# A hybrid attention block: the compressed branch's steps at other slots, and the stream's pieces run in pairs

## The chip, the core and the metric

The kernel runs on one core of one Trainium2 chip. The metric is the device time of one execution in microseconds, as the median of several; a profile of one more execution shows what each engine did. The engines are named as the profile names them: PE (TensorE's matmuls), PEld (its weight loads), DVE (VectorE), ACT (ScalarE), POOL (GpSimd), SP (SyncE, which only issues transfers here).

## The reference, cut to what matters

One layer of a decoder trunk on 512 tokens of width 2048, in float32. A normalised `h` goes through one wide input projection; its columns feed a sparse attention (mixer A) and a gated MLP (mixer B); both are merged, projected and added back. What the change touches is in mixer A, for 16 heads in 4 groups with head size 64:

```
kc, vc = compress(k_c), compress(v_c)            # 31 compressed keys and values per group
sc  = q . kc * scale - slope * distance          # compressed scores, masked
p_c = softmax(sc) ;  o_c = p_c . vc
o_s = softmax(q . k_s ...) . v_s                 # selected blocks: all 8 of them at this length
o_w = softmax(q . k_w ...) . v_w                 # window of 512: all causal keys
o   = gate0 * o_c + gate1 * o_s + gate2 * o_w
```

At 512 tokens the top-16 selection takes all 8 blocks, so the selected and the window branch are both plain causal attention, over different keys and values.

## The kernel before, in words

**Matmuls in three parts.** Each float32 operand is split into a high and a low part (`high` at L158 on ACT, `low` at L164 on DVE), and a product is three matmuls: high by high, low by high, high by low. The large projections are jobs of one generator, `gemm`. One step of it, called a unit or piece of the stream here, is such a triple of 128x512 matmuls (L425 to L427 for the jobs that run during the attention: the query and gate projections `q2` to `q7` and `za0` to `za7`). `fill(n)` runs the next n units.

**The attention** runs over 48 slots: 8 tiles `ft` of two heads each, and in each tile six slots j = 0 to 5, for the query blocks i = 3, 3, 2, 2, 1, 0. Slots 0 to 3 take one branch each, slots 4 and 5 both branches at once. What happens to a slot is spread over four slots: `scores` (L1262, L1263: two pairs of matmuls into two PSUM banks `ps_s`, then on DVE the bias and row maximum at L1266, which empties the bank), `exponentials` on ACT in the same slot (L1275), `weigh` on DVE one slot later (L1286, L1291), `transpose_probs` on PE two slots later (L1316 into `ps_t`, emptied by a cast to `pth` on ACT and a subtraction to `ptl` on DVE), `values` three slots later (L1335, L1336 into `ps_o`).

**The compressed branch** works on a group of four heads, that is on a pair of tiles, one pair ahead. Its steps are events in between: `cmp_keys` (POOL), `cmp_scores` (L1371: two halves of two matmuls, each half in a bank `ps_c`, emptied by a copy on ACT at L1372 and an addition on DVE at L483), `cmp_softmax` (transposes L1383, copy L1386, then DVE and ACT), `cmp_weigh`, `cmp_transpose` (transposes L1413 into `ps_c`, copy `pc` L1415 on ACT, two casts, two subtractions on DVE), and `cmp_values` once per tile (L1425 into `ps_c`, copy `oc` L1427).

**Banks.** PSUM has eight banks here, two for each of four tags. `ps_s` and `ps_c` share the two banks with tag "s"; `ps_t` has the two of "t", `ps_o` those of "o", the stream's jobs those of "g" in this stage. A new tile of a tag takes the bank of the last but one, and its first matmul waits until that one has been emptied.

**The order** is written out by hand. For each slot the main loop (`for s in range(n + 3)`) makes a list of events. PE's events are each preceded by `flush()`, which issues what was deferred (the `low` parts, the additions), and followed by `fill` with a number of units. A running credit sets that number: the units of the attention, 224 less 19, are spread evenly over the events on PE. Each engine runs its own instructions in the order in which they were issued.

## Time and profile before

| | |
|---|---|
| median of 3 runs | 1517.71 us (1517.4 to 1518.03) |
| the profiled execution | 1518.42 us, of it 1516.7 us span |
| granted TensorE clock | 0.999 |
| PE busy | 1504.3 us, 99% of the span |
| DVE, ACT, POOL busy | 1217.1, 853.9, 375.0 us |
| DMA | 340.5 MB, mean 225 GB/s |
| the attention's slots | about 215 to 476 us of the span |

The span is the time from the first to the last instruction; the profiled execution's own time has 1.7 us around it. In a row of the profile's timeline stand the start, the duration and the engine of an instruction, its line and the tiles that it writes and reads, and in brackets how long the engine was idle before it and who ended that. Matmuls overlap: the time that one costs is the distance from its start to the next one's, 0.23 us for 512 columns, not the duration that is printed, 0.39.

### The profile page before, as it was taken

To read this page: it belongs to the slowest core of one execution; us is meant where nothing else is said; L and a number is where in the kernel's file an instruction comes from. 1 tells how busy PE (TensorE), PEld (TensorE's weight loads), DVE (VectorE), ACT (ScalarE), POOL (GpSimd) and SP (SyncE) were. 2 spreads that over 40 slices of the span, in tenths; PEclk is the share of its full clock that TensorE was granted. 3 is DMA by queue.
4 is the path that set the end of the run, shared out by engine and by line. 5 is a ranking of instruction groups with operands and counts; after the bars stand their busy time and mean duration, and the time that the engine had idled before them with its cause. 6 is when DMAs were issued, how large, how long until landed. Compare 5 with 4: busy or idle time off the path is not lost.

```text
span 1516.7 us, 20626 instructions
## 1 busy us (share of the span) xinstructions
PE 1504.3 (99%) x7269; PEld 1262.3 (83%) x7269; DVE 1217.1 (80%) x1871; ACT 853.9 (56%) x1488; POOL 375.0 (25%) x595
## 2 busy tenths in 40 slices
PE   9999999999999999999999999999999999999997
PEld 8889988888888888888888888888888888888886
DVE  7557768899997888978887878797877985677877
ACT  6544456767675555555655555555556565444556
POOL 1311223323432233333333333421110002100000
PEclk9999999999999999999999999999999999999999
DMA  8686879778875895968686968896797879955555
GB/s 314 202 167 198 235 158 217 176 159 224 180 189 194 271 288 139 301 154 282 145 265 177 267 176 263 231 317 250 265 323 245 248 187 330 314 169 182 182 209 191
DMA packets 187351, 340.54 MB, mean 225 GB/s; under 512 B 12520, under 2 KB 84848, under 8 KB 184048
## 3 DMA queue, kind: packets, MB, share of 16 engines
q0 software_dynamic: 67216, 168.42, 41.1%
q1 hardware_dynamic: 119888, 170.55, 35.5%
q8 instruction: 57, 0.93, 0.3%
q14 instruction: 46, 0.38, 0.1%
q10 hardware_dynamic: 144, 0.26, 0.0%
HBM read 278.88 MB, written 109.58 MB: 256 GB/s over the span
## 4 chain that ended last, share of the span: by engine, by line
PE 95%; ACT 2%; DVE 2%; DMA 1%; issue 0%; POOL 0%; DVEq 0%; SPq 0%; ACTq 0%; POOLq 0%
PE ps_m L399 7%; PE ps_m L400 7%; PE ps_m L401 7%; PE ps_wo L400 3%; PE ps_wo L401 3%; PE ps_wo L399 3%; PE ps_t L1316 2%; PE ps_za L427 2%; PE ps_za L425 2%; PE ps_za L426 2%; PE ps_q L425 2%; PE ps_q L427 2%; PE ps_q L426 2%; PE ps_u L399 2%; PE ps_u L401 2%; PE ps_ub L401 2%
## 5 line engine op out<-in xcount | busy, mean ns | idle before, releaser
L164 DVE TENSOR_TENSOR ls<-b,hs 128x1024 fp32r<-128x1024 f32 x218 | 266.5, 1223 | 107.5 <-ACT hs L158 106.4
L158 ACT CAST hs<-b 128x1024 fp32r<-128x1024 f32 x218 | 229.2, 1053 | 195.0 <-PE ps_m L401 43.1
L158 ACT CAST hs<-raw 128x1024 fp32r<-128x1024 f32 x114 | 120.0, 1055 | 116.9 <-issue 34.1
L164 DVE TENSOR_TENSOR ls<-raw,hs 128x1024 fp32r<-128x1024 f32 x114 | 139.3, 1222 | 38.7 <-ACT hs L158 38.5
L164 DVE TENSOR_TENSOR lo<-raw,hi 128x512 fp32r<-128x512 f32 (+1 forms) x152 | 100.8, 669 | 36.9 <-issue 9.9
L158 ACT CAST hi<-raw 128x512 fp32r<-128x512 f32 (+1 forms) x152 | 89.8, 601 | 56.8 <-PE ps_pg L440 10.6
L399 PE MATMUL ps_m<-hs,act_h 128*128 128x512 f32 x256 | 100.2, 391 | 0.0
L400 PE MATMUL ps_m<-ls,act_h 128*128 128x512 f32 x256 | 99.7, 389 | 0.0
L401 PE MATMUL ps_m<-hs,act_l 128*128 128x512 f32 x256 | 99.7, 389 | 0.0
L282 DVE TENSOR_TENSOR b<-raw,b 128x1024 f32<-128x1024 f32 x72 | 87.8, 1219 | 3.0 <-DMA raw<-in_w_in_dram 2.9
L282 DVE TENSOR_TENSOR b<-b,b 128x1024 f32<-128x1024 f32 x72 | 87.7, 1219 | 0.0
L158 ACT CAST pth<-ps_t 128x512 fp32r<-128x512 f32 (+1 forms) x88 | 47.8, 544 | 58.7 <-PE ps_t L1316 58.2
L1275 ACT ACTIVATE prob<-prob,st 128x512 f32<-128x512 f32 (+3 forms) x128 | 70.7, 555 | 2.6 <-DVE st L1266 2.4
L164 DVE TENSOR_TENSOR ptl<-ps_t,pth 128x512 fp32r<-128x512 f32 (+1 forms) x88 | 56.1, 637 | 14.5 <-ACT pth L158 13.8
L358 POOL COPY pad_r<-pad_r 128x1 f32<-128x1 f32 x42 | 31.0, 737 | 136.1 <-ACT pad_r L357 136.1
L1266 DVE CUSTOM_DVE_ANT_0 prob<-ps_s,b 128x512 f32<-128x512 f32 (+3 forms) x128 | 56.2, 485 | 1.9 <-PE ps_s L1263 1.5
L401 PEld LDWEIGHTS ps_m<-hs,act_l 128*128 128x128 f32 x256 | 48.1, 188 | 10.0
L400 PEld LDWEIGHTS ps_m<-ls,act_h 128*128 128x128 f32 x256 | 48.1, 188 | 9.8
L399 PEld LDWEIGHTS ps_m<-hs,act_h 128*128 128x128 f32 x256 | 48.1, 188 | 9.9
L425 PE MATMUL ps_za<-act_h,hi 128*128 128x512 f32 x128 | 53.7, 420 | 0.0
L1291 DVE TENSOR_SCALAR prob<-prob,st,gates 128x512 f32<-128x512 f32 (+3 forms) x128 | 51.5, 455 | 1.8
L425 PE MATMUL ps_q<-act_h,hi 128*128 128x512 f32 x128 | 52.2, 408 | 0.0
(704 smaller groups left out, 4556.4 us busy)
## 6 DMA issues: line engine op xcount, KB each, us to landing
raw<-in_w_in_dram SPq DMA_DIRECT2D x112, 512.0 KB, 5.6
b<-in_w_in_dram SPq DMA_DIRECT2D x56, 512.0 KB, 7.2
o<-in_w_out_dram POOLq DMA_DIRECT2D x48, 512.0 KB, 8.0
t<-in_w_up_b_dram POOLq DMA_DIRECT2D x24, 512.0 KB, 8.1
raw<-in_w_ple_gate_dram SPq DMA_DIRECT2D x24, 512.0 KB, 3.8
b<-o SPq DMA_DIRECT2D x18, 512.0 KB, 6.5
o<-o POOLq DMA_DIRECT2D x16, 512.0 KB, 4.9
act_l<-gate POOLq DMA_DIRECT2D x8, 1024.0 KB, 12.8
```

The costliest lines, as they stand in the source:

```text
L158: nc.scalar.copy(hi, src)
L164: nc.vector.tensor_tensor(out=lo, in0=src, in1=hi.bitcast(F32), op=ALU.subtract)
L282: nc.vector.tensor_tensor(out=b[o], in0=b[x], in1=b[y], op=ALU.subtract)
L399: nc.tensor.matmul(o, ah, wh, start=st, stop=False, skip_group_check=go)
L400: nc.tensor.matmul(o, ah, wl, start=False, stop=False, skip_group_check=go)
L401: nc.tensor.matmul(o, al, wh, start=False, stop=sp, skip_group_check=go)
L425: nc.tensor.matmul(ps, hi[:, j], ah, start=st, stop=False)
L426: nc.tensor.matmul(ps, hi[:, j], al, start=False, stop=False)
L427: nc.tensor.matmul(ps, lo[:, j], ah, start=False, stop=sp)
L1266: nc.vector.tensor_tensor_reduce(out=pt[:, j * n:j * n + n], in0=o[:, j], in1=b0[:, 512 - n:], scale=-SLOPE[h], scalar=3.0e38, op0=ALU.add ...
L1275: nc.scalar.activation(sl, sl, AF.Exp, bias=st[:, 0, j, hh:hh + 1], scale=-1.0, accum_out=st[:, 1, j, hh:hh + 1])
L1291: nc.vector.tensor_scalar(out=sl, in0=sl, scalar1=st[:, 1, j, hh:hh + 1], scalar2=gates[:, i, gate:gate + 1], op0=ALU.mult, op1=ALU.mult)
```

## The change

- `cmp_scores` does one half now (`a` = 0 or 1) and is an event twice: in slot 4 and in slot 5 of an odd tile, where both halves were one event of slot 5. Its work on POOL (`vcb`) goes with the second half.
- `cmp_values` of an even tile is the last event of slot 5, behind the second transposes and values. In odd tiles it stays in slot 3.
- The number of units after an event is no longer the whole part of the credit: below two (and with no `cmp_transpose` next), it is two after the scores if the credit is positive, and none after another event.

```
-    def cmp_scores(g):
-        for ft in (2 * g, 2 * g + 1):
-            finish(f"q{ft}")
-        t = pct_t["s"] = ring(1, F32)[:, 0]
-        halves = slice(0, 64), slice(64, 128)
-        for a in range(2):
-            b = bank("s", "ps_c")
-            for r in range(2):
-                nc.tensor.matmul(b, kcp[:, 32 - 32 * r:160 - 32 * r], qs[4 * g + 2 * a + r], start=r == 0, stop=r == 1)
-            nc.scalar.copy(t[halves[a]], b[halves[1 - a]])
-            deferred.append(partial(add, t[halves[a]], t[halves[a]], b[halves[a]]))
+    def cmp_scores(g, a):
+        finish(f"q{2 * g + a}")
+        if not a:
+            pct_t["s"] = ring(1, F32)[:, 0]
+        t, b, halves = pct_t["s"], bank("s", "ps_c"), (slice(0, 64), slice(64, 128))
+        for r in range(2):
+            nc.tensor.matmul(b, kcp[:, 32 - 32 * r:160 - 32 * r], qs[4 * g + 2 * a + r], start=r == 0, stop=r == 1)
+        nc.scalar.copy(t[halves[a]], b[halves[1 - a]])
+        deferred.append(partial(add, t[halves[a]], t[halves[a]], b[halves[a]]))
+        if a:
+            cmp_parts(g)
+
+    def cmp_parts(g):
         for r in range(4):
...
     cmp_keys(0)
-    for f, u in zip((cmp_scores, cmp_softmax, cmp_weigh, cmp_transpose), (4, 3, 4, 7)):
+    fill(4)
+    flush()
+    cmp_scores(0, 0)
+    for f, u in zip((partial(cmp_scores, a=1), cmp_softmax, cmp_weigh, cmp_transpose), (0, 3, 4, 7)):
...
-            if ft % 2 == 1 and ft < 7 and j == 5:
-                events.append((cmp_scores, (ft + 1) // 2))
+            if ft % 2 == 1 and ft < 7 and j >= 4:
+                events.append((cmp_scores, (ft + 1) // 2, j - 4))
...
-            if j == (3 if ft % 2 else 5):
+            if ft % 2 and j == 3:
                 events.append((cmp_values, ft))
...
         events += tq[1:] + vq[1:]
+        if s < n and ft % 2 == 0 and j == 5:
+            events.append((cmp_values, ft))
...
-                units = max(int(credit) + ahead, e[0] is scores)
+                units = int(credit) + ahead
+                if units < 2 and not ahead:
+                    units = 2 if e[0] is scores and credit > 0 else 0
                 fill(units)
                 credit -= units
```

What this does to the order is seen at three places. In the rows, `x4` counts equal instructions that follow each other; L1369 of the changed kernel is L1371 of the one before, L1370 is L1372, L1415 is L1413, L1417 is L1415 and L1427 is L1425.

**The compressed scores.** PE in slot 5 of tile 1, before, from the first transposes to the second:

```order
L1316 MATMUL ps_t<-ident,prob 128x128 x4
L1335 MATMUL ps_o<-pth,vt 128x256
L1336 MATMUL ps_o<-ptl,vt 128x256
L1335 MATMUL ps_o<-pth,vt 128x256
L1336 MATMUL ps_o<-ptl,vt 128x256
L425 MATMUL ps_q_2913<-act_h_88,hi 128x512
L426 MATMUL ps_q_2913<-act_l_89,hi 128x512
L427 MATMUL ps_q_2913<-act_h_88,lo 128x512
L1371 MATMUL ps_c<-b_2371,kcp 128x512 x2
L1371 MATMUL ps_c<-b_2634,kcp 128x512 x2
L1316 MATMUL ps_t<-ident,prob 128x128 x2
```

PE in slot 4 of tile 1, now, from the unit before the first transposes to the second:

```order
L425 MATMUL ps_za_2637<-act_h_94,hi 128x512
L426 MATMUL ps_za_2637<-act_l_95,hi 128x512
L427 MATMUL ps_za_2637<-act_h_94,lo 128x512
L1316 MATMUL ps_t<-ident,prob 128x128 x4
L1335 MATMUL ps_o<-pth,vt 128x256
L1336 MATMUL ps_o<-ptl,vt 128x256
L1335 MATMUL ps_o<-pth,vt 128x256
L1336 MATMUL ps_o<-ptl,vt 128x256
L1369 MATMUL ps_c<-b_2371,kcp 128x512 x2
L1316 MATMUL ps_t<-ident,prob 128x128 x2
```

The first half has moved from slot 5 to slot 4, and the second half stands the same way in slot 5. The unit between the values and the compressed scores is gone; two units stand between the scores and the first transposes (the second of them is shown), and two behind the second values. ACT at the same place, before (slot 5) and now (slots 4 and 5):

```order
L158 CAST pth<-ps_t 128x512
L1275 ACTIVATE prob,st<-prob,st 128x128 x4
L158 CAST hi<-raw 128x512
L1372 COPY b_2922<-ps_c 64x512 x2
L158 CAST pth<-ps_t 128x256
```

```order
L158 CAST pth<-ps_t 128x512
L1275 ACTIVATE prob,st<-prob,st 128x256 x4
L1370 COPY b_2856<-ps_c 64x512
L158 CAST pth<-ps_t 128x256
L611 ACTIVATE o_580<-ps_za_2637 128x512
L158 CAST hi<-raw 128x512
L158 CAST pth<-ps_t 128x512
L1275 ACTIVATE prob,st<-prob,st 128x128 x4
L1370 COPY b_2856<-ps_c 64x512
L158 CAST pth<-ps_t 128x256
```

The copies stand alone now, each directly behind the slot's four exponentials; the cast of weights (`hi<-raw`) that stood between is elsewhere in the slot.

**The compressed probabilities' transposes.** PE in slot 4 of tile 4, from these transposes on, before and now:

```order
L1413 MATMUL ps_c<-ident,b_3737 128x128 x4
L1316 MATMUL ps_t<-ident,prob 128x128 x2
L1335 MATMUL ps_o<-pth,vt 128x256
L1336 MATMUL ps_o<-ptl,vt 128x256
L1335 MATMUL ps_o<-pth,vt 128x256
L1336 MATMUL ps_o<-ptl,vt 128x256
L425 MATMUL ps_q_3999<-act_h_90,hi 128x512
L426 MATMUL ps_q_3999<-act_l_91,hi 128x512
L427 MATMUL ps_q_3999<-act_h_90,lo 128x512
L1262 MATMUL ps_s<-ob_h,b_3174 128x256
```

```order
L1415 MATMUL ps_c<-ident,b_3656 128x128 x4
L1316 MATMUL ps_t<-ident,prob 128x128 x2
L1335 MATMUL ps_o<-pth,vt 128x256
L1336 MATMUL ps_o<-ptl,vt 128x256
L1335 MATMUL ps_o<-pth,vt 128x256
L1336 MATMUL ps_o<-ptl,vt 128x256
L1262 MATMUL ps_s<-ob_h,b_3174 128x256
```

The unit behind the last values is gone; it stands ahead of the slot's first transposes now.

**The compressed values of an even tile.** PE in slot 5 of tile 4, before, from the compressed values to the next slot's scores, and now, from the same values on:

```order
L1425 MATMUL ps_c<-b_4091,vcb 128x512 x2
L425 MATMUL ps_q_3999<-act_h_92,hi 128x512
L426 MATMUL ps_q_3999<-act_l_93,hi 128x512
L427 MATMUL ps_q_3999<-act_h_92,lo 128x512
L1316 MATMUL ps_t<-ident,prob 128x128 x2
L1335 MATMUL ps_o<-pth,vt 128x256
L1336 MATMUL ps_o<-ptl,vt 128x256
L425 MATMUL ps_q_3999<-act_h_92,hi 128x512
L426 MATMUL ps_q_3999<-act_l_93,hi 128x512
L427 MATMUL ps_q_3999<-act_h_92,lo 128x512
L1262 MATMUL ps_s<-ob_h,b_3448 128x512
```

```order
L1335 MATMUL ps_o<-pth,vt 128x256
L1336 MATMUL ps_o<-ptl,vt 128x256
L1427 MATMUL ps_c<-b_4091,vcb 128x512 x2
L1262 MATMUL ps_s<-ob_h,b_3448 128x512
L1263 MATMUL ps_s<-ob_l,b_3448 128x512
L1262 MATMUL ps_s<-ob_h,b_3448 128x512
```

Two units, the second transposes and the values now stand ahead of the compressed values, and the next slot's scores directly behind them.

## The prediction

> **What bounds the kernel now.** I read the page first, then the stretch of the attention, then its waits, then the order of events at the places that the waits name.
>
> ```profile
> span 1516.7 us, 20626 instructions
> PE 1504.3 (99%) x7269; PEld 1262.3 (83%) x7269; DVE 1217.1 (80%) x1871; ACT 853.9 (56%) x1488; POOL 375.0 (25%) x595
> ```
>
> TensorE sets the end: it has work in 99% of the span, and the change neither adds nor removes one of its instructions. It moves instructions only inside the attention, which is this stretch:
>
> ```profile
> 215.00:476.00 261.00, 259.37 (x1476) 220.99 (x1476) 234.50 (x650) 180.98 (x482) 90.27 (x129) 1.00 0.81 187
> ```
>
> The columns are the stretch, its length, and the busy time of PE, PEld, DVE, ACT and POOL. PE is full, VectorE has 234.5 of 261 us, ScalarE 181. So the change can win only what PE loses here by waiting, and it can lose by making PE wait more. Where PE loses time, and what ScalarE waits for:
>
> ```profile
> ACT pth L158 <- PE ps_t L1316: 58.2, 31, 2.8
> PEld ps_s L1262 <- DVE b L483: 3.0, 6, 0.6
> PE ps_c L1425 <- DVE st L1266: 0.9, 3, 0.3
> ```
>
> The second and third row are the places: six waits of the scores (L1262) for the additions that empty the compressed scores' bank (L483), and three of the compressed values (L1425) for a bank that the scores before them still hold. All are waits for one of the two banks with tag "s". The first row matters most for the change: ScalarE's cast of transposed probabilities is first in its queue in a slot, and it waits for PE's transposes.
>
> One of the three places of the first kind, in order of time. "Zero" below is always the start of the first stream unit after a slot's scores.
>
> ```profile
> 268.52 0.27 PE L1262 MATMUL ps_s<-ob_h,b 128*128 128x256 f32 x1
> ...
> 268.98 0.40 PE L425 MATMUL ps_za<-act_h,hi 128*128 128x512 f32 x1
> 269.69 0.60 PE L1316 MATMUL ps_t<-ident,prob 128*128 128x128 f32 x4
> 270.38 0.59 ACT L158 CAST pth<-ps_t 128x512 fp32r<-128x512 f32 x1
> 270.60 0.39 PE L425 MATMUL ps_q<-act_h,hi 128*128 128x512 f32 x1
> 270.86 0.41 ACT L1275 ACTIVATE prob<-prob,st 128x128 f32<-128x128 f32 x1
> 271.29 1.09 PE L1371 MATMUL ps_c<-b,kcp 128*128 128x512 f32 x4
> 272.22 0.38 PE L1316 MATMUL ps_t<-ident,prob 128*128 128x128 f32 x2
> 272.41 0.60 ACT L158 CAST hi<-raw 128x512 fp32r<-128x512 f32 x1
> 273.04 1.19 ACT L1372 COPY b<-ps_c 64x512 f32<-64x512 f32 x2
> 273.66 1.40 DVE L483 TENSOR_TENSOR b<-b,ps_c 64x512 f32<-64x512 f32 x2 [0.22 <-ACT b L1372]
> 273.83 0.39 PE L427 MATMUL ps_q<-act_h,lo 128*128 128x512 f32 x1
> 274.40 0.50 PE L1262 MATMUL ps_s<-ob_h,b 128*128 128x512 f32 x1 [0.18 <-DVE b L483]
> 275.12 0.50 PE L1262 MATMUL ps_s<-ob_h,b 128*128 128x512 f32 x1
> 275.69 0.40 PE L425 MATMUL ps_q<-act_h,hi 128*128 128x512 f32 x1
> ```
>
> The reader sees a chain on ScalarE that hangs on PE's transposes: zero 268.98, transposes +0.71, cast +1.40, first exponential +1.88, the four of 128 columns over at +3.43 (0.39 each), a cast of weights, the copies at +4.06, the first addition at +4.68. The scores start 0.74 us after an addition has started (273.66 to 274.40; they were due 0.34 earlier, since 273.83 + 0.23 = 274.06). From 273.83 to 275.69 PE takes 1.86 us for one matmul and four of 0.23, that is 1.15: 0.71 us lost.
>
> **What the change moves, and what each piece costs.** Steps on PE between zero and later events are read off these rows: one stream unit 0.69 (three matmuls of 0.23), the first transposes and the values after them 0.91 (269.69 to 270.60; 0.35 + 0.09 is the transposes' part), a half of the compressed scores 0.46 (271.29 to 272.22 for two), two transposes 0.22, the short values 0.23, the long ones 0.47, a pair of scores 0.46 at 128 columns (268.52 to 268.98), 0.92 at 512. From transposes to cast 0.69, from cast to exponentials 0.48.
>
> *Pairing of the units.* The bare gain of fewer changes between kinds of matmul is nothing to count: a unit's last matmul takes the same 0.23 whether values, scores or another unit follow. What does change: after the scores now two units run before the transposes, not one. PE's slot is not longer for it, but the cast starts at 1.38 + 0.69 = +2.07 instead of about +1.40, and everything behind it in ScalarE's queue is 0.69 later, while the next slot's scores are due when they were. In a plain slot this is covered: the scores' two banks are emptied by VectorE a slot ahead, and the transposes' banks come round a slot later. Where ScalarE empties an "s" bank, nothing covers it. These places follow.
>
> *Compressed scores, now half in slot 4, half in slot 5 (three times).* Slot 4: cast +2.07, exponentials +2.55, four of 256 columns in 1.99 (next fence, 363.68 to 365.67), so the copy goes at +4.54, now directly behind them; addition 0.62 later, +5.16; bank free for the scores 0.74 later, +5.90. The scores that need it are the second of slot 5: 0.91 + 0.46 + 0.22 + 0.47 + four units 2.76 + 0.23 = +5.05. Wait 0.85, and 0.1 for starting again (274.40 + 0.23 against the 0.33 that it took): 0.95. Slot 5: exponentials end at 2.55 + 1.55 = +4.10, addition +4.72, free +5.46; due 0.91 + 0.46 + 0.22 + 0.23 + 2.76 + 0.46 = +5.04: 0.42 + 0.1 = 0.52. Together 1.47 where 0.71 was lost; three times, **+2.3 us**. Each wait is for one copy and one addition now, not two, but there are two of them. PE runs in order, so the rest of the slot stands behind each, and ScalarE and VectorE wait for it in turn. Behind the first addition on VectorE stand the low parts of the second transposes and the next slot's maxima; the maxima start with the late scores anyway, so that is covered by the same wait.
>
> *The compressed probabilities' transposes (L1413), not moved by name, but moved by the pairing (three times).* They take an "s" bank that ScalarE copies out:
>
> ```profile
> 361.82 0.40 PE L425 MATMUL ps_q<-act_h,hi 128*128 128x512 f32 x1
> 362.51 0.60 PE L1316 MATMUL ps_t<-ident,prob 128*128 128x128 f32 x4
> 363.20 0.59 ACT L158 CAST pth<-ps_t 128x512 fp32r<-128x512 f32 x1 [2.09 <-PE ps_t L1316]
> 363.68 0.51 ACT L1275 ACTIVATE prob<-prob,st 128x256 f32<-128x256 f32 x1
> 364.79 0.60 PE L1413 MATMUL ps_c<-ident,b 128*128 128x128 f32 x4
> 365.67 0.60 ACT L158 CAST hi<-raw 128x512 fp32r<-128x512 f32 x1
> 366.18 0.58 ACT L1415 COPY pc<-ps_c 128x512 f32<-128x512 f32 x1
> 366.73 0.28 PE L1263 MATMUL ps_s<-ob_l,b 128*128 128x256 f32 x1
> 366.85 0.34 PE L1262 MATMUL ps_s<-ob_h,b 128*128 128x256 f32 x1
> ```
>
> Here the chain ends in a dead heat: the copy starts at +4.36 and the second scores start 0.67 later, at +5.03, as soon as PE gets to them. Moving the cast from +1.38 to +2.07 makes that a wait of 0.66 to 0.69, with the restart 0.75, at the two later places (same units, same weights' cast in the queue). At the first place (tile 2) that cast is out of the way (0.51 less), but the unit that stood behind the transposes is gone as well: free at 2.55 + 1.99 + 0.67 = +5.21, due 1.38 + 0.91 + 0.69 + 0.44 + 0.22 + 0.47 + 0.23 = +4.34, 0.87 and 0.1. Together 2.5 against 0.1 to 0.2 now: **+2.3 us**.
>
> *The compressed values of even tiles, now last in slot 5 (three times).* Before:
>
> ```profile
> 369.21 0.39 PE L427 MATMUL ps_q<-act_h,lo 128*128 128x512 f32 x1
> 369.27 0.28 DVE L1266 CUSTOM_DVE_ANT_0 prob<-ps_s,b 128x128 f32<-128x128 f32 x1
> 369.92 0.71 PE L1425 MATMUL ps_c<-b,vcb 128*128 128x512 f32 x2 [0.31 <-DVE st L1266]
> 370.46 0.40 PE L425 MATMUL ps_q<-act_h,hi 128*128 128x512 f32 x1
> ...
> 306.72 0.57 ACT L1427 COPY oc<-ps_c 128x512 f32<-128x512 f32 x1
> ...
> 283.55 0.71 ACT L1275 ACTIVATE prob<-prob,st 128x512 f32<-128x512 f32 x1
> ```
>
> 369.21 to 370.46 is 1.25 us for 0.69 of work: 0.56 lost, because VectorE is late with the maxima. At the slot's end that wait is gone (three times 0.56, -1.7). But now the next scores come directly behind, and the second of them needs the same bank that the values have just filled. ScalarE's queue: exponentials end +4.10, cast of the second transposes 0.36, cast of weights 0.51, copy 0.57 and the 0.08 to the release: +5.62. Due 1.38 + 0.91 + 0.22 + 1.38 + 0.23 + 0.46 + 0.46 = +5.04. Wait 0.58, with the restart 0.68; three times +2.0. Net **+0.3 us**.
>
> *The rest.* The starting steps ahead of the slots keep PE's order. In odd tiles the compressed values stand as far from zero as they did (two units, transposes, values). POOL's and SP's queues keep what they issue. The softmax transposes of the third tile pair come later in their slot: 2.55 + 1.42 for two exponentials of 512 columns (0.71 in the last row) + 0.51 + 0.65 against a due time of +4.93, about 0.2.
>
> **Sum**: +2.3 + 2.3 + 0.3 + 0.2 = +5.1 us on the profiled execution's 1518.4 us (its span is 1516.7), so 1523.5. That execution lies 0.7 above the median of 1517.7, so I forecast **1522.8 us**.
>
> Bounds: the gain cannot exceed what PE loses at the places, 3 x 0.71 + 3 x 0.56 and the small ones of about 0.5, so 4.3 us. Each of the new waits is the difference of two times of about 5 us, at twelve places; 0.1 us off in ScalarE's chain is 1.2 us in the sum. I take 0.25 as the error of a chain put together from parts (the cast of weights counts 0.51 and may stand on either side): 3 us either way.
>
> A rule that speaks for the pairing: the Trainium skill, Perfetto Trace Analysis, section Matmul Optimizations, says that the array's power follows its use, so matmuls ought to run back to back in batches. The trace leaves it nothing to win: the granted clock of the stretch is 1.00 above, with the singles. By the rule the sum would stay as it is, since what it asks for is granted already.
>
> **The rivals.**
>
> *The waits vanish (faster).* Half the compressed scores per slot, and values that no longer meet late maxima: if every release came before its due time, PE would gain up to 4.3 us, about 1513.7. For it: the values' wait does go, and the copy loses the second copy ahead of it. Against it: it needs ScalarE's chain to start at +1.40 as before, and the first fence of waits shows the chain's head waiting for the transposes 31 times. It decides at a chain 0.7 us shorter than in my sum. 8%.
>
> *A draw.* The chain runs 0.4 us shorter than I put it, say because the casts of weights fall into the wait for the transposes everywhere. Then the scores' waits come to 0.55 and 0.12, the transposes' to 0.57 and twice 0.35, the values' to 0.28: 2.0 + 1.3 + 0.8 = 4.1 against 4.0 now, about 1518. For it: these casts move between slots in the changed order. Against it: I have put each one where the order has it. 24%.
>
> *VectorE becomes the bound (slower still).* It is 90% busy here, and with the second cast later it idles ahead of the low parts and catches up in the next slot. Around the softmax of even tiles it has the reductions on top; if its lateness then reaches the transposes' banks, by up to the 0.69 us that the chain is later, in one or two slots of each of three tile pairs, another 2 to 4 us come on top: 1526. For it: 26.5 us of slack over 48 slots is 0.55 each, less than 0.69. Against it: the banks come round a slot later. 10%.
>
> **How the numbers follow.** The likeliest, 58%, has its own range 1519.8 to 1525.8. A change of 0.2% is 3.0 us, about what a measurement of this kernel tells from none. One tenth of the likeliest case falls inside that; of the draw, one tenth lies beyond it on either side; of the first rival an eighth stays inside. Slower: 0.52 + 0.02 + 0.10 = 0.64; within: 0.06 + 0.19 + 0.01 = 0.26; faster: 0.07 + 0.03 = 0.10. The range from 1516.3 to 1526.5 takes in the draw, the bounds and half of the third rival.
>
> **What would show it.** In the changed profile's waits: the scores (L1262) wait for the compressed scores' addition six times, in slots 5 and 0, about 0.85 and 0.4 each; they wait for ScalarE's copies pc and oc, which they do nowhere now; the compressed values no longer wait for the maxima. In order of time the first cast of a slot starts 2.07 us after zero. If the pc and oc copies release nobody, the chain on ScalarE is not what binds, and the first rival holds. If the transposes wait for the low parts in many slots, the third does. If PE's loss in the stretch stays near 4 us, it is the draw.

## The result, and the profile after

| | before | after |
|---|---|---|
| median | 1517.63 us (6 runs, 1517.4 to 1518.03) | 1528.77 us (6 runs, 1528.22 to 1529.39) |
| ratio | | 1.0074, 95% interval 1.0063 to 1.0084 |
| the profiled execution, its span | 1518.42, 1516.7 us | 1528.22, 1526.4 us |
| granted clock | 0.999 | 0.998 |
| PE's loss in the attention (215 to 487 us) | 4.35 us | 16.29 us |

The change costs 11.1 us; I had forecast 5.1 and a range that ends at 1526.5. "Loss" here and below is worked out from PE's rows as in the prediction: the distance from the start of a matmul to the start of the next, less the time that its columns take (0.23 us for 512), added up where it is above 0.035. By places:

| PE waits at | before | my sum | after |
|---|---|---|---|
| the scores behind the compressed scores (add) | 2.3 | 4.4 | 5.1 |
| the scores behind the compressed probabilities' transposes (`pc`) | 0.1 | 2.5 | 2.9 |
| the scores behind the even tiles' compressed values (`oc`) | 0 | 2.0 | 1.9 |
| the even tiles' compressed values (maxima) | 1.7 | 0 | 0 |
| the softmax transposes of the third pair | 0 | 0.2 | 0.3 |
| the transposes, for a low part (`ptl`) | 0.2 | 0.2 | 4.3 |
| the odd tiles' compressed values (maxima) | 0 | 0 | 1.8 |
| small ones | 0.1 | 0.1 | 0.1 |

By the pages of the two profiles PE is busy for 1505.2 us (1504.3 before), so the work is the same; the 9.7 us of span are waiting, and the chain of work that sets the end runs over ScalarE and VectorE for 4% of the span each where it was 2% each (PE 89% for 95%). PE's loss grew by 11.9 us, the attention from its first scores to its last values by 11.0 (262.4 to 273.4 us); in these two executions the stretch ahead of it was 1.0 us shorter after the change, the stretch behind it 0.3. The waits of PE in the attention of the changed kernel:

```profile
PE ps_s L1262 <- DVE b L483: 3.5, 6, 0.8
PE ps_t L1316 <- DVE ptl L164: 3.1, 4, 1.0
PE ps_s L1262 <- ACT pc L1417: 2.0, 3, 0.9
PE ps_s L1262 <- ACT oc L1429: 1.0, 3, 0.4
PE ps_c L1427 <- DVE st L1266: 0.9, 3, 0.5
```

The first, third and fourth row are the waits of my sum, six, three and three as said. The second and the last are not in it. The fences below show rows picked from a view, in order of time; the rows between them are left out. A place of the first kind, the changed kernel in slot 4 of tile 3:

```profile
331.79 0.39 PE L425 MATMUL ps_za<-act_h,hi 128*128 128x512 f32 x1
333.85 0.59 ACT L158 CAST pth<-ps_t 128x512 fp32r<-128x512 f32 x1 [2.60 <-PE ps_t L1316]
334.33 0.51 ACT L1275 ACTIVATE prob<-prob,st 128x256 f32<-128x256 f32 x1
336.43 0.58 ACT L1370 COPY b<-ps_c 64x512 f32<-64x512 f32 x1
337.05 0.68 DVE L483 TENSOR_TENSOR b<-b,ps_c 64x512 f32<-64x512 f32 x1 [1.89 <-ACT b L1370]
337.79 0.39 PE L1262 MATMUL ps_s<-ob_h,b 128*128 128x256 f32 x1 [0.79 <-DVE b L483]
```

Zero is 331.79, the cast starts at +2.06 (forecast +2.07), the copy at +4.64 (forecast +4.54), the addition at +5.26 (+5.16). VectorE stands idle for 1.89 us ahead of the addition: it is not VectorE that is late there, but what it is given.

The wait that I had put at nothing, the compressed values of an odd tile (slot 3 of tile 3). Before:

```profile
321.43 0.60 PE L1316 MATMUL ps_t<-ident,prob 128*128 128x128 f32 x4
322.57 0.34 PE L1262 MATMUL ps_s<-ob_h,b 128*128 128x384 f32 x1
322.68 0.68 DVE L164 TENSOR_TENSOR lo<-raw,hi 128x512 fp32r<-128x512 f32 x1
322.91 0.59 ACT L158 CAST pth<-ps_t 128x512 fp32r<-128x512 f32 x1
323.28 0.41 DVE L1351 TENSOR_TENSOR o<-o,ps_o 64x256 f32<-64x256 f32 x1
324.16 0.69 DVE L164 TENSOR_TENSOR ptl<-ps_t,pth 128x512 fp32r<-128x512 f32 x1
324.76 0.55 DVE L1266 CUSTOM_DVE_ANT_0 prob<-ps_s,b 128x384 f32<-128x384 f32 x1
325.56 0.63 PE L1425 MATMUL ps_c<-b,vcb 128*128 128x512 f32 x2
```

and after:

```profile
324.24 0.60 PE L1316 MATMUL ps_t<-ident,prob 128*128 128x128 f32 x4
324.59 0.42 PE L1262 MATMUL ps_s<-ob_h,b 128*128 128x384 f32 x1
325.22 0.41 DVE L1351 TENSOR_TENSOR o<-o,ps_o 64x256 f32<-64x256 f32 x1 [0.18 <-ACT o L1348]
325.74 0.58 ACT L158 CAST pth<-ps_t 128x512 fp32r<-128x512 f32 x1
326.10 0.69 DVE L164 TENSOR_TENSOR lo<-raw,hi 128x512 fp32r<-128x512 f32 x1
326.82 0.69 DVE L164 TENSOR_TENSOR ptl<-ps_t,pth 128x512 fp32r<-128x512 f32 x1
327.43 0.55 DVE L1266 CUSTOM_DVE_ANT_0 prob<-ps_s,b 128x384 f32<-128x384 f32 x1
328.04 0.72 PE L1427 MATMUL ps_c<-b,vcb 128*128 128x512 f32 x2 [0.20 <-DVE st L1266]
```

The first row of each is the *second* transposes of the slot before. They stood 1.14 us ahead of the next scores, with a unit in between; now they stand 0.35 ahead. Their cast starts 0.34 us after the scores' start before, 1.15 after. But their low part (`ptl`) does not follow the cast directly: in both kernels VectorE first makes two additions on `o` (L1351, L1352), for which ScalarE copies `o`. These start 0.71 us after the scores' start before and 0.63 now, so they are not late. What is new ahead of `ptl` is the low part of weights (`lo<-raw,hi`, 0.7 us): it stood ahead of the additions, at +0.11, and now stands behind them, at +1.51. So `ptl` starts at +2.23 for +1.59, and the maxima, which stand behind it in VectorE's queue, at +2.84 for +2.19. The compressed values are due at about the same distance as before (2.99, now 3.1), but the bank comes free later: 0.46 us lost.

### The profile page after: what moved, and what is told of

Read it like the earlier page. It is cut to its first block, busy times and chain, and to the rows that moved or that the text cites. A ratio compares the mean times of both kernels' runs of the same rounds, so it can differ in the third digit from the quotient of the medians.

```text
span 1526.4 us, 20639 instructions
## 1 busy us (share of the span) xinstructions
PE 1505.2 (99%) x7269; PEld 1262.3 (83%) x7269; DVE 1220.2 (80%) x1871; ACT 856.1 (56%) x1488; POOL 379.4 (25%) x595
## 4 chain that ended last, share of the span: by engine, by line
PE 89%; ACT 4%; DVE 4%; DMA 1%; issue 1%; POOL 0%; DVEq 0%; ACTq 0%; POOLq 0%
PE ps_m L400 7%; PE ps_m L399 7%; PE ps_m L401 7%; PE ps_wo L400 3%; PE ps_wo L401 3%; PE ps_wo L399 3%; ACT prob L1275 2%; PE ps_u L401 2%; PE ps_ub L399 2%; PE ps_u L400 2%; PE ps_pg L401 2%; PE ps_pg L399 2%; PE ps_ua L400 2%; PE ps_zb L400 2%; PE ps_zb L399 2%; PE ps_vn L400 2%
## 5 line engine op out<-in xcount | busy, mean ns | idle before, releaser
L164 DVE TENSOR_TENSOR ls<-b,hs 128x1024 fp32r<-128x1024 f32 x218 | 266.6, 1224 | 107.8 <-ACT hs L158 106.8
L164 DVE TENSOR_TENSOR ls<-raw,hs 128x1024 fp32r<-128x1024 f32 x114 | 139.4, 1223 | 39.2 <-ACT hs L158 38.9
L164 DVE TENSOR_TENSOR lo<-raw,hi 128x512 fp32r<-128x512 f32 (+1 forms) x152 | 101.1, 670 | 37.4 <-issue 8.7
L358 POOL COPY pad_r<-pad_r 128x1 f32<-128x1 f32 x42 | 34.4, 820 | 132.3 <-ACT pad_r L357 132.3
L164 DVE TENSOR_TENSOR ptl<-ps_t,pth 128x512 fp32r<-128x512 f32 (+1 forms) x88 | 55.5, 637 | 13.4 <-ACT pth L158 12.2
L1316 PE MATMUL ps_t<-ident,prob 128*128 128x128 f32 x320 | 49.5, 274 | 3.1 <-DVE ptl L164 3.1
```

Source lines behind the costliest of these rows:

```text
L164: nc.vector.tensor_tensor(out=lo, in0=src, in1=hi.bitcast(F32), op=ALU.subtract)
L358: nc.gpsimd.tensor_copy(steps[:, 16 + i:17 + i], steps[:, i:i + 1])
L1316: nc.tensor.transpose(b[:, (2 * e + hh) * P:(2 * e + hh + 1) * P], pts[hh][:, c:c + P], ident)
```

## The experiments

All ratios stand against the kernel before as measured beside each run (1517.6 to 1517.9 us). "Tile pair" is two tiles, 12 slots.

| run | what differs | median us | PE's loss us |
|---|---|---|---|
| before | | 1517.63 | 4.35 |
| after | | 1528.77 | 16.29 |
| e1 | pairs alone | 1526.09 | 13.85 |
| e2 | moved steps alone | 1519.57 | 5.97 |
| e3 | after, exponentials ahead of the first transposes | 1526.07 | 13.21 |
| e4 | before, the same | 1522.28 | 8.87 |
| e5 | before, one unit first, the rest in pairs | 1522.08 | 8.93 |
| e6 | before, two units first, the rest single | 1523.67 | 10.89 |
| e7 | before, even tiles' values last | 1517.39 | 4.05 |
| e8 | moved steps, compressed scores in "t" banks | 1519.14 | 5.73 |
| e9 | after, copies ahead of the exponentials | 1527.90 | 15.42 |
| e10 | moved steps, copies ahead of the exponentials | 1518.73 | 5.28 |
| e11 | before, copies ahead of the exponentials | 1517.47 | 3.94 |
| e12 | after, less VectorE work at the softmax | 1525.98 | 13.00 |
| e13 | after, less VectorE work in each slot | 1525.71 | 13.30 |
| e14 | before, the same | 1517.38 | 3.92 |
| e15 | after, as e9 and e13 together | 1522.64 | 10.39 |
| e16 | before, more ScalarE work in each slot | 1521.95 | 8.48 |
| e17 | after, weight casts on GpSimd | 1525.14 | 13.01 |
| e18 | before, weight casts on GpSimd | 1514.79 | 1.30 |

### Which part of the change costs

**e1, the pairs alone**

```
-                units = max(int(credit) + ahead, e[0] is scores)
+                units = int(credit) + ahead
+                if units < 2 and not ahead:
+                    units = 2 if e[0] is scores and credit > 0 else 0
```

> The kernel before, with the new rule for the stream's pieces alone (two at a time, none in between); the compressed steps stay where they were. Theory A (the pairing makes the first transposes of a slot about 0.69 us later, and with them ScalarE's cast, exponentials and copies and VectorE's second low part): the waits at the compressed scores and at the compressed probabilities' transposes are there, and the transposes wait for the low parts; PE loses 12 to 16 us in the attention where it lost 4.35, so about 1525 to 1529 us. Theory B (the other places of the compressed steps are what costs): PE loses 4 to 6 us, 1517 to 1520 us. Theory C (the two costs need each other): in between, 1520 to 1524 us.

Measured: 1526.09 us, ratio 1.0055 (1.0042 to 1.0067).

**e2, the moved steps alone** (the change with these lines taken back)

> The changed kernel with the old rule for the pieces (one behind the scores, the rest one at a time); the compressed scores stay spread over two slots and the even tiles' compressed values stay last in theirs. Theory A: the first cast of a slot starts about 1.4 us after the slot's first scores, each half of the compressed scores waits 0.3 us at most, the even tiles' values wait no more for the maxima; PE loses 1 to 4 us, so 1514.5 to 1517.5 us. Theory B: the places cost by themselves, PE loses 10 us or more, 1523 to 1528 us. Theory C: 1518 to 1522 us.

Measured: 1519.57 us, ratio 1.0011 (1.0002 to 1.0020). **e7**, of the moves only the even tiles' values:

```
-            if j == (3 if ft % 2 else 5):
+            if ft % 2 and j == 3:
                 events.append((cmp_values, ft))
...
         events += tq[1:] + vq[1:]
+        if s < n and ft % 2 == 0 and j == 5:
+            events.append((cmp_values, ft))
```

> The kernel before with one part of the change alone: the even tiles' compressed values last in their slot. From the run with all the moves (PE loses 5.97, of it 1.23 at the copies behind these values and 3.96 at the spread scores): the three waits for the maxima (1.65 with their small ends) go, three waits for the copy of about 0.45 come, PE loses 3.9 to 4.2, 1517 to 1518.2 us. Then the spread of the compressed scores alone is worth +1.5 to +2 us. If the two moves need each other's lateness, this one comes out below 1516.5 or above 1518.5.

Measured: 1517.39 us, ratio 0.9996 (0.9987 to 1.0005).

The pairs cost 8.2 us, the moves 1.7, together 9.9 of the 11.1. Of the moves the values' place is worth nothing that can be measured (three waits of 0.55 for three of 0.43 to 0.49), so the spread of the compressed scores is what costs, about 2. My expectation for e2 (0.3 us a half) was wrong: in slot 4 the halves still wait 0.84 to 1.15 us, because in front of the copy stand the cast, four exponentials of 256 columns (2.0 us, 1.55 in slot 5) and a cast of weights; two halves wait where both halves together waited once.

### What about the pairs

**e5, one unit behind the scores, the rest in pairs**, and **e6, two behind the scores, the rest single** (both with the compressed steps where they were):

```
+                units = int(credit) + ahead
+                if e[0] is scores:
+                    units = 1
+                elif units < 2 and not ahead:
+                    units = 0
```

```
-                units = max(int(credit) + ahead, e[0] is scores)
+                units = max(int(credit) + ahead, 2 * (e[0] is scores))
```

> The kernel before, compressed steps where they were, with one piece behind the scores as before and all other pieces in pairs or threes. It tells apart whether pairs as such cost, or the second piece between the scores and the first transposes. Theory A (the second piece ahead of the first transposes): the first cast of a slot starts 1.4 us after the slot's first scores, as before; PE loses 3.5 to 5.5 us in the attention (4.35 before, 13.85 with all pieces in pairs), 1517 to 1519 us. Theory D (pieces in pairs are what costs, wherever they stand): PE loses 9 to 14 us, 1522 to 1526 us.

> The other half: the kernel before with two pieces behind the scores and the rest one at a time. Theory A: first cast at 2.07 us, the waits at the compressed probabilities' transposes (about 0.8 to 1.2 each) and the transposes' waits for the low parts (about 1.2 in tiles 2 and 4) are there; PE loses 11 to 15 us, 1524 to 1527 us. Theory D: one pair a slot of two, so a half of the loss at most: 7 to 9 us, 1520 to 1522 us.

Measured: 1522.08 (1.0027, 1.0016 to 1.0038) and 1523.67 (1.0035, 1.0022 to 1.0049). Neither theory is right alone. PE's waits in e5 and in e6:

```profile
PE ps_t L1316 <- DVE ptl L164: 2.1, 3, 0.7
PE ps_s L1262 <- DVE st L1266: 1.2, 1, 1.2
```

```profile
PE ps_t L1316 <- DVE ptl L164: 2.4, 2, 1.4
PE ps_s L1262 <- DVE b L483: 2.4, 3, 1.0
PE ps_c L1425 <- DVE st L1266: 2.0, 4, 1.1
```

In e6 the first cast is late, and the compressed scores lose 0.9 to 1.6 us each. But the odd tiles' compressed values lose 0.05 at most, where e1 and the changed kernel lose 0.46 to 0.75 in three tiles: with single units there is still a unit behind the second transposes at a slot's end. (The last row is the even tiles' values, 0.54 to 0.56 each as before, and 1.3 in tile 0.) In e5 the first cast is on time and these values lose 0.1 at most, but the second transposes of three slots lose 0.9 each: they stand directly behind the values, where a unit stood between, so PE is there about 0.7 us earlier than the low part allows. The scores behind the compressed probabilities' transposes lose 0.75 at the two later places, where the unit behind the last values is gone. (2.2 of the 4.6 us that e5 adds are lost in the first three slots of the attention, the one row of 1.2 us above, where this edit leaves a unit out.) So pairs cost in two ways: one unit more ahead of the first transposes, and one less behind or ahead of the second ones.

There is a third way, in tile 0, and only in runs with two units ahead of the first transposes: a cast of weights waits for its transfer and holds up ScalarE's queue. In the changed kernel:

```profile
235.92 0.62 ACT L158 CAST hi<-raw 128x512 fp32r<-128x512 f32 x1 [4.66 <-DMA raw<-in_w_in_dram]
239.29 0.43 DVE L164 TENSOR_TENSOR ptl<-ps_t,pth 128x256 fp32r<-128x256 f32 x1 [1.54 <-ACT pth L158]
239.77 0.44 PE L1316 MATMUL ps_t<-ident,prob 128*128 128x128 f32 x2 [0.73 <-DVE ptl L164]
```

The slot's casts and exponentials stand behind that cast, VectorE idles for the second of them, and PE loses 0.96 us. In e1, e3, e6, e9, e13 and e15 the same cast waits 4.2 to 4.7 us and PE loses 0.7 to 1.4; in the kernel before and in the runs with one unit there it waits 0.5 at most, and PE loses nothing at this place. Why the transfer comes late for the pairs is not shown.

### Is it the exponentials' place in ScalarE's queue

**e3 and e4**, in the changed kernel and in the one before:

```
-        events += tq[:1]
         if s < n:
             events.append((exponentials, s))
+        events += tq[:1]
```

> The changed kernel with the exponentials of a slot issued ahead of the first transposes, so that on ScalarE they stand ahead of the cast of those transposes and no longer behind it. Theory A: ScalarE's copies come 0.4 to 0.7 us earlier after the slot's start, so the three kinds of copy waits (5.1, 2.9 and 1.9 us in the changed kernel) lose half or more of their size; the cast of the first transposes comes up to 0.5 us later, so the low parts' lateness (3.9 us) stays or grows. About 1521 to 1526 us. Theory B (what costs is not ScalarE's chain but where the steps stand on PE): unchanged, 1527.5 to 1530 us.

> The kernel before with the same swap: exponentials ahead of the first transposes. Theory A: with single pieces the transposes are done shortly after the exponentials could start, so ScalarE's chain gains little at its head; the three waits of 0.71 us at the compressed scores fall by 0 to 0.5 us each, the three of 0.56 us at the compressed values stay. 1515.5 to 1518 us. A rival: the later cast makes the low parts late on VectorE and the transposes wait for them: 1519 to 1523 us.

Measured: 1526.07 us (2.7 less than the change) and 1522.28 (4.4 more than before, 1.0030, 1.0018 to 1.0042). In e3 the first halves of the compressed scores lose at most 0.1 us instead of 1.05, and the transposes' copies 0.08 instead of 0.9 and 0.75 at two places; but the second halves lose 0.75 still, the third transposes' copy 1.67, the even tiles' values 0.91 each for 0.62, and the waits for low parts grow from 4.3 to 4.8. e4 fell out as its rival says: the cast behind the exponentials makes the low part late, the transposes (1.6 us) and the odd tiles' values (1.4) wait. One queue has both: the copies and the casts that VectorE needs. What goes first makes the other late.

**e9, e10, e11**, the other order: exponentials behind the compressed step, so that the copy is made as soon as the bank is full (in e9 for both halves of the compressed scores and the compressed probabilities' transposes, in e10 and e11 for the compressed scores):

```
-        if s < n:
+        late = s < n and (ft % 2 == 1 and ft < 7 and j >= 4 or ft % 2 == 0 and ft > 0 and j == 4)
+        if s < n and not late:
             events.append((exponentials, s))
...
+        if late:
+            events.append((exponentials, s))
```

> The changed kernel, with the exponentials of three slots per tile pair issued behind the compressed step (both halves of the compressed scores, the compressed probabilities' transposes) and not ahead of it, so that ScalarE makes the copy as soon as TensorE has filled the bank. Theory A (ScalarE's queue is what makes these copies late): the copy starts when the matmuls end, the waits of the next scores (5.14 us at the scores' additions, 2.86 us at the transposes' copy) go down to 0 to 0.3 each; the exponentials end 0.6 to 1.3 us later and the second cast with them, which may add up to 2 us in waits for the low parts; PE loses 8.5 to 10.5 us, 1520.5 to 1523.5 us. Rival (VectorE's lateness sets the end, and whatever is won at the copies is lost at the transposes' banks): 1525 to 1529 us.

> All moves with single pieces, with the same swap at the two halves of the compressed scores. Theory A: of the 5.97 us that PE loses the 3.96 at these halves go, 0 to 1 us comes back at the low parts; 2 to 3 us lost, 1515 to 1516.7 us, faster than the kernel before. Rival: 1517.5 to 1520 us.

> The kernel before with the same swap at its compressed scores (two copies together, then the exponentials, which end about 1.2 us later in the slot). Theory A: the three waits of 0.71 to 0.87 us, 2.29 in all, go, up to 1.2 us comes back at the low parts in the next slot; 1515.4 to 1517 us. Rival: the later exponentials reach the next slot's first transposes: 1517.5 to 1519.5 us.

Measured: 1527.90, 1518.73 and 1517.47 us. Theory A was wrong on all three sizes: waits went where I said, and came back behind. In e10 the first halves wait no more and the second lose 1.0 to 1.3 us where they lost 0.43 to 0.47; in e11 one of the three waits falls from 0.71 to 0.37, the others stay. e9 at the compressed probabilities' transposes of tile 2:

```profile
302.10 0.59 ACT L1417 COPY pc<-ps_c 128x512 f32<-128x512 f32 x1 [1.01 <-PE ps_c L1415]
306.38 0.42 DVE L164 TENSOR_TENSOR ptl<-ps_t,pth 128x256 fp32r<-128x256 f32 x1 [1.55 <-ACT pth L158]
306.86 0.44 PE L1316 MATMUL ps_t<-ident,prob 128*128 128x128 f32 x2 [1.32 <-DVE ptl L164]
```

The copy starts when the bank is full and the scores wait no more. But the exponentials and with them the second cast start later, VectorE waits 1.55 us for it, and the next transposes lose 1.5 us. The three first halves and the three copies, 5.8 us, are gone in e9; PE's loss falls by 0.9.

**e8, another bank**: the halves of the compressed scores (with all moves, single units) take a "t" bank:

```
-        t, b, halves = pct_t["s"], bank("s", "ps_c"), (slice(0, 64), slice(64, 128))
+        t, b, halves = pct_t["s"], bank("t", "ps_c"), (slice(0, 64), slice(64, 128))
```

> All moves with single pieces, but each half of the compressed scores goes into a bank of the transposes' pair instead of one of the scores' pair; the same matmuls, copies and additions. Theory A': the copy and the addition are exposed only because the next scores need the bank they empty; then the six waits (3.96 us) vanish, the next slot's first transposes come later than the addition and wait 0.2 us at most, PE loses 1.5 to 2.5 us, 1514.5 to 1516.5 us: faster than both kernels. Rival: the second transposes of the slot or the first of the next then wait for the low parts or for the same copy, 0.3 us and more at each of six places, 1517.5 to 1520 us.

Measured: 1519.14 us, ratio 1.0006 (0.9998 to 1.0015): the scores behind them wait no more, the transposes do, 1.0 to 1.5 us at three places. Its rival was right in its first form: a half takes one of the two "t" banks, so the next transposes need the one that the transposes before them filled, and they wait for its low part (`ptl`, L164 releases them at all three places), not for the copy.

### VectorE's load or ScalarE's queue

**e12** leaves out the bias, the maxima and their subtraction of the compressed softmax (and makes the exponentials' scale tiny):

```
         def shift():
-            nc.vector.tensor_tensor(out=c, in0=c, in1=c0..., op=ALU.add)
-            nc.vector.tensor_reduce(out=st[:, 0], in_=c, axis=AX.X, op=ALU.max)
-            nc.vector.tensor_tensor(out=c, in0=c, in1=st[:, 0]..., op=ALU.subtract)
             deferred.append(exps)
```

> The changed kernel without the three VectorE operations ahead of the compressed softmax's exponentials (the bias, the maxima and their subtraction are left out, and the exponentials' scale is made tiny to keep them finite), 2.0 us less on VectorE at three places; nothing else. It asks whether VectorE's lateness there is what the first transposes of the next slots wait for. Theory A: the two waits for the low parts at the softmax of tiles 2 and 4 (1.26 and 1.22 us) go, the others stay; 1525.8 to 1527 us. Rival (the low part is late only because ScalarE's cast is): nothing changes, 1528 to 1529.5 us.

Measured: 1525.98 us, 2.8 less than the change. The waits for low parts in tile 2 (1.26) and in tile 0 (0.95) are gone, that in tile 4 (1.22) is 0.98. (The expectations give all these waits together as 3.9 us, without the 0.06 of each restart.) Tile 0 has no compressed softmax in its slots: there the transfer of weights was in time in e12, whose first scores start 1.3 us later than in the changed kernel's profile. So the long VectorE stretch is the cause in tile 2 and has a small part in tile 4. The rows of the changed kernel in tile 2 agree: the cast is done at 294.15, and VectorE, busy without a gap, comes to the low part at 294.82.

```profile
291.35 0.33 PE L1262 MATMUL ps_s<-ob_h,b 128*128 128x384 f32 x1
293.56 0.59 ACT L158 CAST pth<-ps_t 128x512 fp32r<-128x512 f32 x1
294.82 0.69 DVE L164 TENSOR_TENSOR ptl<-ps_t,pth 128x512 fp32r<-128x512 f32 x1
```

**e13, e14, e15** leave out `weigh`'s multiplications in each slot (`for j in range(nb)` is `for j in range(0)`), in the changed kernel, in the one before, and in e9:

> The changed kernel without VectorE's multiplications of the probabilities by the reciprocal sums and gates (left out; the outputs are then not the reference's), about 0.9 to 1.4 us less on VectorE in each slot. Theory S (ScalarE's queue in the slots with compressed steps is full, so its later start is what those slots lose): the waits for the low parts and the odd tiles' values go (5.6 us), the waits for copies stay within 0.2 us each; PE loses 8 to 11 us in the attention. Theory V (VectorE's load): all of it goes, PE loses under 4 us.

> The kernel before with the same multiplications left out. Theory S: the waits for the maxima go (1.65 us), those at the compressed scores stay mostly (2.3 us, of which up to 0.3 each may be VectorE's queue); PE loses 1.5 to 2.7 us, and the changed kernel without them is 6 to 9 us slower than this one. Theory V: the two differ by less than 2 us.

> The changed kernel with the copies ahead of the exponentials and without the multiplications. Theory S: the slots with the compressed probabilities' transposes hold 5.5 to 6 us of ScalarE work behind a first cast that starts 2.1 us into the slot, so the second cast is late whatever VectorE does: the transposes' waits of about 1.5 us there (three of them) stay, PE loses 6 to 9 us. Theory V: with room on VectorE the earlier copies gain what they were meant to, PE loses under 3 us.

Measured: 1525.71, 1517.38 and 1522.64 us. With VectorE relieved by some 50 us the change still costs 8.3 us of its 11.1, and PE loses 13.30 where theory S said 8 to 11. PE's waits in e13:

```profile
PE ps_s L1262 <- DVE b L483: 3.5, 6, 0.8
PE ps_t L1316 <- DVE ptl L164: 1.6, 2, 1.0
PE ps_s L1262 <- ACT pc L1417: 1.6, 3, 0.6
PE ps_s L1262 <- ACT oc L1429: 1.0, 3, 0.4
PE ps_c L1427 <- DVE st L1266: 0.6, 3, 0.2
```

The copies' waits are what they were within 0.1 us, but for one of 0.45, as theory S said. Against it, more than half of the others stayed too (low parts 2.1 of 4.3, odd tiles' values 1.4 of 1.8); and in e14 the even tiles' values, which I expected to wait no more, still lose 0.55 each. They name VectorE as the one that releases, but VectorE itself stood idle a little earlier, for ScalarE: in e14 for its casts of the compressed probabilities, in e13 at tile 3 for its copy of `o`.

```profile
301.63 1.40 DVE L164 TENSOR_TENSOR b<-pc,b 64x512 fp32r<-64x512 f32 x2 [2.38 <-ACT b L158]
```

```profile
324.52 0.41 DVE L1351 TENSOR_TENSOR o<-o,ps_o 64x256 f32<-64x256 f32 x1 [1.27 <-ACT o L1348]
325.40 0.69 DVE L164 TENSOR_TENSOR lo<-raw,hi 128x512 fp32r<-128x512 f32 x1
326.12 0.69 DVE L164 TENSOR_TENSOR ptl<-ps_t,pth 128x512 fp32r<-128x512 f32 x1
```

From the copy on, VectorE works without a gap: two additions, the low part of weights, the low part of the probabilities, the maxima. So the wait at this place is a relay, ScalarE's copy and then the order of VectorE's queue. The multiplications that e13 leaves out stood ahead of the idle time, which only grows without them (1.27 us for 0.18).

In e15 the waits at the compressed scores and at the compressed probabilities' copies are gone; the transposes' waits of 1.5 to 1.6 us at the three places of e9 stay. Relieving VectorE makes the earlier copies worth 2.9 us (13.30 to 10.39) where they were worth 0.9; the 10.39 are more than the 6 to 9 expected.

**e16, ScalarE late in the kernel before**: a copy of 424 columns onto itself behind each slot's first cast.

```
+    late_t = att.tile([P, 424], F32, tag="late", name="late", bufs=1)
+    nc.gpsimd.memset(late_t, 0.0)
...
         split(hi[:, :w], lo[:, :w], b[:, :w], later=True)
+        if bi == 0:
+            nc.scalar.copy(late_t, late_t)
```

> The kernel before with one more ScalarE instruction in each slot, a copy of 424 columns onto itself, behind the cast of the first transposes: about 0.5 us, after which the exponentials and all copies come later; the first low part does not. Theory S: waits of 0.3 to 0.5 us more at each compressed step whose bank the next scores want (three pairs of compressed scores, the transposes twice), and at the second transposes; the plain slots lose nothing, since ScalarE waits 1.9 us a slot for the transposes. PE loses 6.5 to 9 us, 1520 to 1523 us. Theory V: VectorE starts its first low part as before, so little changes: 4.5 to 6 us lost, 1517.5 to 1519.5 us.

Measured: 1521.95 us, ratio 1.0027 (1.0016 to 1.0037), 4.2 us for one instruction of 0.55 us a slot. PE's waits:

```profile
PE ps_s L1264 <- DVE b L483: 2.0, 3, 0.8
PE ps_t L1318 <- DVE ptl L164: 0.9, 2, 0.6
PE ps_s L1264 <- ACT pc L1419: 0.7, 3, 0.2
```

The places of the changed kernel are back, with no unit moved: compressed scores 1.15 to 1.3 us each (0.7 to 0.9 before), the transposes' copy 0.5 each, and 1.6 in all at the low parts, although the first cast of a slot is as early as before: only the second stands behind the added copy.

**e17, e18, ScalarE relieved with nothing left out**: the casts of the stream's weights go to GpSimd during the attention, in the changed kernel and in the one before.

```
+            if job.kind == "T" and state["slot"]:
+                nc.gpsimd.tensor_copy(hi, src)
+            else:
+                high(hi, src)
-            high(hi, src)
```

> The changed kernel with the casts of the stream's weights on GpSimd during the attention; the same numbers are computed. Theory S (ScalarE's queue behind the late first cast): 0.6 us less in each slot ahead of the copies, so each wait at the compressed scores, the compressed probabilities' transposes and the even tiles' values falls by 0.4 to 0.6 us; of 16.3 us PE loses 6 to 10 us, 1518.5 to 1523 us, if GpSimd makes the casts in time. Rival: GpSimd's queue, which waits up to 3.9 us for transfers in places, makes the casts late and the stream's pieces wait for them: 1528 us or more.

> The kernel before with the same casts on GpSimd. Theory S: the waits at the compressed scores (2.3 us) fall by 0.4 to 0.6 us each, those for the maxima stay or shrink; PE loses 2 to 3 us, 1515.5 to 1517 us, faster than the kernel before. Rival (GpSimd late): 1519 us or more.

Measured: 1525.14 us (3.6 less than the change, less than I expected) and 1514.79 us, ratio 0.9982 (0.9972 to 0.9991), **2.8 us faster than the kernel before**, and faster than both. PE's loss in the attention is 1.30 us there: the waits at the compressed scores are 0.2 to 0.4 us, those of the compressed values 0.17 at most. The copies that started 4.06 us after zero start at 3.55. In e17 the six waits at the compressed scores stay, and the rows show why:

```profile
332.50 0.59 ACT L158 CAST pth<-ps_t 128x512 fp32r<-128x512 f32 x1 [2.60 <-PE ps_t L1319]
335.09 0.58 ACT L1373 COPY b<-ps_c 64x512 f32<-64x512 f32 x1
```

Cast to copy is 2.59 us, as in the changed kernel (333.85 to 336.43, 2.58): no cast of weights stood in between there. What is lost at that place hangs on the start of the first cast and the exponentials behind it, not on the weights.

e17 also tells whether the late second cast is what the odd tiles' values wait for. At the place in tile 3:

```profile
323.24 0.42 PE L1265 MATMUL ps_s<-ob_h,b 128*128 128x384 f32 x1
323.86 0.59 ACT L158 CAST pth<-ps_t 128x512 fp32r<-128x512 f32 x1
325.47 0.69 DVE L164 TENSOR_TENSOR ptl<-ps_t,pth 128x512 fp32r<-128x512 f32 x1
```

The cast starts 0.62 us after the scores' start, 0.53 earlier than in the changed kernel. The low part starts at +2.23 as there, and the same 0.46 us are lost: the low part of weights still stands ahead of it on VectorE. In tile 0 the late transfer now holds up GpSimd and not ScalarE, and the 0.96 us are gone.

## Why the prediction was half right

- **The chain's later start**: right. The first cast at +2.06 for +2.07, ScalarE waiting for the transposes ahead of it, and waits at just the three kinds of copies that the sum named. Direction and the main mechanism stand; e1 and e6 show that it is the units ahead of the first transposes, e16 that 0.55 us on ScalarE alone makes the same waits.
- **The compressed scores**: 4.4 forecast, 5.1 measured, 0.1 a place. Four exponentials of 256 columns take 2.10 us up to the next instruction (334.33 to 336.43), not the 1.99 that I took from a place where a cast follows; those of 128 columns 1.67, not 1.55.
- **The compressed probabilities' transposes**: 2.5 forecast, 2.9 measured (0.97, 0.75 and 0.75 against 0.91, 0.75 and 1.20, so the third place was mis-sized); the even tiles' values 2.0 and 1.9; the softmax transposes 0.2 and 0.3.
- **"In a plain slot this is covered: ... the transposes' banks come round a slot later"**: this step failed. 4.3 us are lost there where 0.2 were. I followed the first transposes, and not the second ones. At the two largest places PE wants their bank at nearly the same distance from the slot's scores as before (3.0 us for 3.1 in tile 2, 3.1 for 3.0 in tile 4), but the low part that frees it starts at +3.47 for +2.39 in tile 2 and at +3.50 for +2.25 in tile 4. What makes it late differs from place to place. In tile 2 (1.26 us) it is VectorE's own queue: the cast is done 0.67 us before the low part starts, and the wait goes in e12 and in e13. In tile 4 (1.22) it is the relay from ScalarE's copy of `o` through VectorE's queue: e12 leaves 0.98, e13 1.18. In tile 0 (0.96) it is the transfer of weights; most of the rest is the last slot (0.58).
- **"In odd tiles the compressed values stand as far from zero as they did"**: true of PE, and not the question; the step failed by putting this wait at nothing. Their bank is released by VectorE's maxima; 1.8 us are lost. At the place in tile 3 the maxima came 0.65 us later because the low part of weights had moved ahead of the low part that they stand behind; e17 shows that the later cast is not the reason.
- **The third rival** had the first of these as VectorE's load, with 10% and 2 to 4 us. The place and the size were right; the cause was right in tile 2 only: with VectorE relieved, half of the 4.3 us stay (e13). With this rival the sum comes to 1526; the odd tiles' values and 0.1 us at each place make the rest.
- **"The bare gain of fewer changes between kinds of matmul is nothing to count"**: it is about 1 us. The attention grew by 11.0 us and the loss by 11.9; in e1 by 8.4 and 9.5, in e5 by 3.8 and 4.6, while with single units the two agree (e2 1.7 and 1.6, e16 4.1 and 4.1). Most of it lies within the units, in steps from one matmul to the next that are each longer by less than the 0.035 us that the loss counts from. It is a tenth of the loss that the pairs add.
- **Bounds**: "0.1 us off in ScalarE's chain is 1.2 us" held (0.7 at the scores, 0.4 at the transposes). I took 3 us either way as the error of the sum, but that counted only the places already in it.

Of the signs that I named, the compressed values that "no longer wait for the maxima" was wrong: the even ones don't, the odd ones now do. What stays open is why the transfer of weights comes late in tile 0 with two units first, and how the 1.22 us in tile 4 divide between the copy of `o` and VectorE's own work behind it.

## What to carry to other kernels

When a change moves an engine's instructions, follow every group that moves to the end of its release, not only the ones ahead of it: a step next to a slot's end hands its lateness to the next slot. A wait that names an engine as its releaser says little until one has looked at what that engine itself waited for in the rows before, and at what stands ahead in its queue: here a low part of weights, which the change does not name, came to stand ahead of a release. And where waits only change places (the swap of the copies, another bank), take work off the queue that all of them share; here 48 casts on an idle engine gained what no order did.

## What the runs showed of the hardware

GpSimd makes these casts nearly as fast as ScalarE: e18's row and the one before.

```profile
L319 POOL CAST hi<-raw 128x512 fp32r<-128x512 f32 x48 | 33.0, 689 | 68.3 <-PE ps_q L429 25.5 <-PE ps_za L429 17.3 <-issue 14.3
```

```profile
L158 ACT CAST hi<-raw 128x512 fp32r<-128x512 f32 x48 | 29.6, 617 | 0.9 <-PE ps_q L426 0.9
```

Some of VectorE's instructions get a little longer beside them: from before to e18 the low parts of the weights go from 699 to 725 ns (49 of them) and the multiplications from 455 to 475 (128), in all 3.7 us of VectorE, far less than the 29.6 us that ScalarE is freed of. The low parts of the probabilities, which read PSUM, stay at 685 (72). In e18 the low parts of weights that lie beside a GpSimd instruction for more than half of their time take 802 ns (18), those beside none 680 (27). The Trainium skill, Perfetto Trace Analysis, section Optimizing Scalar/DVE Operations, says that GpSimd and VectorE share a read port, so that moving work between those two might not help. The trace agrees that VectorE is slowed, by 4% on these instructions; the work came from ScalarE here, and moving it helped.
